# Routing over 112 sums, bank copies in runs of four, a third buffer for late rows, and three unused tiles

## The chip, the cores and the metric

The kernel runs on one core of a Trainium2 chip. A core has a matrix engine (TensorE, PE in the profile, with its weight loads as PEld), VectorE (DVE), ScalarE (ACT), GpSimd (POOL) and SyncE (SP, which here only issues DMAs), an on-chip memory SBUF of 128 partitions, and PSUM with eight banks for matmul results. Sixteen DMA engines move data between HBM and SBUF. The metric is the time of one execution on the device, in microseconds.

## The reference

One layer of a streaming encoder over 512 frames and 16 leading meta tokens, model width 2048: two attention branches (a latent attention with 8 heads and a stick-breaking attention with 8 heads), gated, merged and added to the input; then a layer of 16,384 tiny experts (PEER), a residual add and a final norm. The change touches the expert layer. For each token:

```python
q = (xb @ w_q).reshape(PEER_BLOCK, PEER_HEADS, 2, PEER_HALF)
s = jnp.einsum('thcd,hcnd->thcn', q, sub_keys).astype(jnp.float32)
s1, i1 = lax.top_k(s[:, :, 0], PEER_TOPK)
s2, i2 = lax.top_k(s[:, :, 1], PEER_TOPK)
cand_s = (s1[..., :, None] + s2[..., None, :]).reshape(PEER_BLOCK, PEER_HEADS, -1)
cand_i = (i1[..., :, None] * PEER_NKEYS + i2[..., None, :]).reshape(PEER_BLOCK, PEER_HEADS, -1)
top_s, top_pos = lax.top_k(cand_s, PEER_TOPK)
idx = jnp.take_along_axis(cand_i, top_pos, axis=-1)
g = jax.nn.softmax(top_s, axis=-1).reshape(PEER_BLOCK, -1)
h = jnp.einsum('tkd,td->tk', u[idx], xb)
act = (g * jax.nn.gelu(h.astype(jnp.float32), approximate=False)).astype(xb.dtype)
return jnp.einsum('tk,tkd->td', act, v[idx])
```

Both lists of 16 come sorted. A sum of places a and b (counted from 0) has (a+1)(b+1) sums that are at least as large, itself included. So a sum with a >= 4 and b >= 4 has at least 25 of them and need not be looked at; 4 x 16 + 12 x 4 = 112 sums are left.

## The kernel before

**Matmuls in three parts.** All weights and activations are fp32. `wtile` (line 213) loads a weight tile `wr` (128 partitions x 1024) on SP's DMA queue, rounds it on ACT into `wh` (line 223) and takes the rest on DVE into `wl` (line 224). Activations are kept split in the same way (`xh`/`xl`, `yh_`/`yl_`, `mgh`/`mgl`, `hgh`/`hgl`, `vah`/`val`). `mm3` (lines 235 to 237) issues three matmuls for each product, in which a 128x128 piece of the weight tile is the stationary operand. `wr` has four buffers, `wh` and `wl` three each, with one more pair for every fourth tile in the last two stages (`more["pool"]`).

**Stages.** First the projections of x with 512 or 264 columns (xh), then the attentions; the branch outputs (line 771, on yh_a and yh_b, 512 columns); the output projection (line 809, on mgh, 512 columns), which leaves `hgh`/`hgl`; the query projection for routing (line 960, on hgh, 512 columns), with the scores and the top 16 of each 128 (`top16`, line 859). Then the experts, and here the 512 tokens are treated in two ways. For 342 of them (ND) all 16,384 experts are computed densely: in `for e in range(NK)` (line 1213, 128 blocks of 48 matmuls with 342 columns) the products with u, and after it, by `STEPS` (line 1292), the products with v. Which experts count is laid on by a table of gates. For the other 170 tokens the chosen rows of u and v are gathered: 128 tokens have one partition each, and 42 tokens three partitions each.

**Rows.** `send` (line 1142) issues one gather of 128 rows of 2048 floats on POOL's queue, `row_step` (line 1163) lets DVE multiply such a row with the tokens and sum (for u, line 1171), or scale and add it (for v, line 1175). There are 171 u rows and 171 v rows, numbered through. `rows_due` (line 1207) issues row steps in pace with the position in the u loop, by the table

```python
PACE = (2, 14, 60, 124, NK - 0.5), (0, 10, 75, 173.5, NU)
```

so 173.5 rows are due at block 124 and NU = 179 at the end. `lead` says how many rows beyond the current one may have been sent: 4 or 6 in most of the loop, 2 from row 166 (OWN - 4) on. Up to row 169 the rows rotate through the buffers of three tags (rows, hin, gin); from row 170 (OWN) on only the two of `rw` are left, since hin and gin then hold the first groups of the v stage. In the v stage, every third row gets a tile of another pool (`gs["pool"]`), and the lead is 3.

**Routing and gates.** `route` (line 887) works through one tile of 128 tokens: sums (line 897), the best 16 of 256 for each head (line 901), and twice, for the two halves of the position, a one-hot comparison, a product and a sum (lines 909 to 913). It is a generator; each `yield` is a point where other work is issued. One token tile is routed under the scores (`early`, line 930, nine steps after every fourth block), three under the u loop (`routing`, line 1105). `gates_of` (line 1038) then builds, token by token, a 128 x 128 table of gates on TensorE (line 1074); `gate_out` (line 1082) copies four tokens of a PSUM bank with two ACT instructions (line 1095) into `gb`, from where POOL's queue stores it to DRAM. The v stage reads it back as `gin` and multiplies it to the stored `hin` (`gated`, line 1199).

**Order.** A scheduler orders each engine's instructions when the program is built. Instructions of one engine start in that order, so a DVE instruction that waits for a gather holds all later ones, the `wl` of line 224 among them.

Of the kernel before, what the change touches and what calls it, by code (L numbers as in the profile page):

```python
# [22 lines left out]
P = 128  # L23
# [39 lines left out]
def _constants():  # L63
    p = np.arange(P)
    cols = {
        "ident": np.eye(P),
        "ones": np.ones((P, P)),
        "tri": (p[:, None] >= p[None, :]),
        "perm": (p[:, None] == (p[None, :] ^ 32)),
        "neg": np.where(p[None, :] <= p[:, None], NEG, 0.0),  # L70
        "qlo": np.where(p[None, :] < 64, 1.0, 0.0) * np.ones((P, 1)),
        "negrow": np.full((P, 64), NEG),
        "freq": (10000.0 ** (-((p % 32) / 32.0)))[:, None],
        "sign": np.where(p % 64 < 32, -1.0, 1.0)[:, None],
        "iota": np.arange(TOPK)[None, :] * np.ones((P, 1)),
        "sel": (p[:, None] // RB == np.arange(NB)[None, :]),
        "eps": np.full((P, 1), EPS),
        "halfpi": np.full((P, 1), math.pi / 2),
    }
    out = []  # L80
    for part in range(2):
        arrs, o = [], 0
        for k, v in cols.items():
            if (k in MIXER_CONST) == bool(part):
                v = np.asarray(v, np.float64).astype(np.float32)
                CONST[k] = (part, o, o + v.shape[1])
                o += v.shape[1]
                arrs.append(v)
        out.append(np.ascontiguousarray(np.concatenate(arrs, axis=1)))
    return out  # L90
# [106 lines left out]
def body(tc, nc, a, dbg=None):  # L197
# [55 lines left out]
    gn = cp.tile([P, 56], F32, name="gn")  # L253
    SP.dma_start(gn, a["gains"])
    csts = [cp.tile([P, CONST_ARR[0].shape[1]], F32, name="cst")]

    def C(k):
        return csts[CONST[k][0]][:, CONST[k][1]:CONST[k][2]]
# [501 lines left out]
    for n, y in (("a", ya), ("b", yb)):  # L760
        yh_ = sp2.tile([P, H, SEQ], F32R, name=f"yh_{n}")
        yl_ = sp2.tile([P, H, SEQ], F32R, name=f"yl_{n}")
        for h in range(H):
            split(yh_[:, h], yl_[:, h], y[:, h])
        ys.append((yh_, yl_))
    mixer.close()
    merge = ExitStack()
    bp = merge.enter_context(tc.tile_pool(name="merge", bufs=1, side="left"))
# [25 lines left out]
    hgl = hgp.tile([P, KC, SEQ], F32R, name="hgl")  # L794
    rh_ = hgp.tile([P, SEQ], F32, name="rh_")
    gr_last = hgp.tile([P, 2, P], F32, name="gr_last")
    rcol = hgp.tile([P, 1], F32, name="rcol")
    rcolb = hgp.tile([P, 1], F32, name="rcolb")

# [53 lines left out]
    eob = rp.tile([P, KB], I32, name="eob")  # L853
    stage = ExitStack()
    rk = stage.enter_context(tc.tile_pool(name="rank", bufs=1, side="right"))
    v1 = rk.tile([P, 4, 16, TOPK], F32, name="v1")
    i1 = rk.tile([P, 4, 16, TOPK], U32, name="i1")

    def top16(vals, idx, src, n):
        wk = rk.tile([P, n], F32, name="wk", tag=f"wk{n}")  # L860
# [13 lines left out]
    def spread_rows():  # L874
# [9 lines left out]
        SP.dma_start(eob[:PB], eob_d.rearrange("t (r k) -> (t r) k", r=RB))  # L884
        SP.dma_start(gwb[:PB], gwb_d.rearrange("t (r k) -> (t r) k", r=RB))

    def route(ti, n, pool):
        shp = [P, n, TOPK, TOPK]
        tv = pool.tile([P, H, TOPK], F32, name="tv", bufs=1)
        ef = keys[ti] = pool.tile([P, 2, H, TOPK], F32, name="ef", bufs=1)  # L890
        for h0 in range(0, H, n):
            hs = slice(2 * h0, 2 * (h0 + n))
            vv, ii = (t[:, ti, hs].rearrange("p (h c) k -> p h c k", c=2) for t in (v1, i1))
            i1f = pool.tile([P, n, 2, TOPK], F32, name="i1f", bufs=1)
            V.tensor_copy(i1f, ii)
            cand = pool.tile([P, n, TOPK, TOPK], F32, name="cand", bufs=1)
            V.tensor_tensor(cand, vv[:, :, 0, :, None].to_broadcast(shp), vv[:, :, 1, None, :].to_broadcast(shp), ALU.add)
            yield
            tp = pool.tile([P, n, TOPK], U32, name="tp", bufs=1)
            for h in range(n):  # L900
                top16(tv[:, h0 + h], tp[:, h], cand[:, h].rearrange("p a b -> p (a b)"), 256)
                yield
            for c, (op_, arg) in enumerate(((ALU.logical_shift_right, 4), (ALU.bitwise_and, 15))):
                pu = pool.tile([P, n, TOPK], U32, name="pu", bufs=1)
                pf = pool.tile([P, n, TOPK], F32, name="pf", bufs=1)
                V.tensor_scalar(pu, tp, arg, None, op_)
                V.tensor_copy(pf, pu)
                oh = pool.tile([P, n, TOPK, TOPK], F32, name="oh", tag="cand", bufs=1)
                V.tensor_tensor(oh, pf[:, :, :, None].to_broadcast(shp), iota[:, None, None, :].to_broadcast(shp), ALU.is_equal)
                yield  # L910
                V.tensor_tensor(oh, oh, i1f[:, :, c, None, :].to_broadcast(shp), ALU.mult)
                yield
                V.reduce_sum(ef[:, c, h0:h0 + n], oh, axis=AX.X)
                yield
        e_ = pool.tile([P, H, TOPK], F32, name="e_", bufs=1)
        V.scalar_tensor_tensor(e_, ef[:, 0], float(NK), ef[:, 1], ALU.mult, ALU.add)
        ev = e_.rearrange("p h k -> p (h k)")
        if ti == 3:
            V.tensor_copy(eo, ev)
        gw = gw_all[:, ti].rearrange("p (h k) -> p h k", k=TOPK)  # L920
        V.tensor_tensor(gw, tv, tv[:, :, :1].to_broadcast(sh2), ALU.subtract)
        S.activation(gw, gw, AF.Exp)
        sm = pool.tile([P, H], F32, name="gsum", bufs=1)
        V.reduce_sum(sm, gw, axis=AX.X)
        V.reciprocal(sm, sm)
        V.tensor_tensor(gw, gw, sm[:, :, None].to_broadcast(sh2), ALU.mult)
        if ti == NT - 1:
            V.tensor_copy(er, ev)

    early = route(3, 2, rk)  # L930
    with tc.tile_pool(name="score", bufs=2, side="left") as sp_, \
# [9 lines left out]
        def scores(hc, qh, ql):  # L941
            ps = ps_tile()
            skh, skl = sk["now"]
            s = slice(hc % 8 * P, (hc % 8 + 1) * P)
            for ti in range(4):
                t = slice(ti * P, (ti + 1) * P)
                mm3(ps[:, t], qh[:, t], ql[:, t], skh[:, s], skl[:, s], True, True)
            sc = sp_.tile([P, 4, NK], F32, name="sc")
            S.activation(sc, ps.rearrange("p (t n) -> p t n", n=NK), AF.Copy)
            for ti in (3, 2, 0, 1):  # L950
                top16(v1[:, ti, hc], i1[:, ti, hc], sc[:, ti], NK)
            if hc % 4 == 3:
                for _ in range(9):
                    next(early, None)

        late = []
# [77 lines left out]
    def after_gelu(ins):  # L1034
        if "gelu" in more:
            tc.add_manual_dep(ins.ins, more["gelu"].ins.name, NOSYNC, reason="not before its block")
# [45 lines left out]
    def gate_out(hold=3):  # L1082

        for _ in range(min(2, len(banks))):
            if banks[0][1] % TB == 0 and len(banks) < hold:
                return
            ps, tok, w = banks.pop(0)
            b, o = tok // TB, tok % TB
            if o == 0:
                gb["now"] = [vi.tile([P, NK // 2, TB], F32, name="gb", tag="gin") for _ in range(2)]  # L1090
                if ND - tok < TB:
                    for half in gb["now"]:
                        G.memset(half[:, :, ND - tok:], 0.0)
            for hf, half in enumerate(gb["now"]):
                after_gelu(S.activation(half[:, :, o:o + w].rearrange("p i t -> p t i"),
                                        ps.rearrange("p (t f i) -> p f t i", t=4, f=2)[:, hf, :w], AF.Copy))
                if o + w == TB or tok + w == ND:
                    for q in range(2):
                        g0 = hf * NG // 2 + q * NG // 4
                        G.dma_start(g_d[g0:g0 + NG // 4, :, b].rearrange("g p j t -> p g (j t)"),  # L1100
                                    half[:, q * NK // 4:(q + 1) * NK // 4].rearrange("p (g j) t -> p g (j t)", j=GRP))
# [2 lines left out]

    def routing():
        for ti in (2, 0, 1):
            yield from route(ti, 2, rk)
            routed.append(ti)
            while routed:
                yield  # L1110
# [31 lines left out]
    def send():  # L1142
# [5 lines left out]
            tag = ("rows", "hin", "gin")[(n - gs["six"]) % 3]  # L1148
        else:
            tag = ("rows", "hin")[n % 2] if n < OWN else "rows"  # L1150
        if tag != "rows":
            row = vi.tile([P, D], F32, name="row", tag=tag)
        elif gs["pool"] is not None and n % 3 == 0:
            row = gs["pool"].tile([P, D], F32, name="row", bufs=1)
        else:
            row = rw.tile([P, D], F32, name="row")
# [50 lines left out]
    def rows_due(pos):  # L1207
        while gs["done"] < np.interp(pos, PACE[0], PACE[1]):
            n = gs["done"]
            row_step(more["lo"], 6 if gs["six"] is not None and gs["six"] + 4 <= n < OWN - 6 else 4 if n < OWN - 4 else 2)  # L1210

    more["pool"] = stage.enter_context(tc.tile_pool(name="weights_u", bufs=1, side="left"))
    for e in range(NK):
# [162 lines left out]
```

## Time and profile before

| | us |
|---|---|
| median of 3 runs | 3620.9 (3619.91 to 3624.22) |
| the profiled execution | 3625.05 |
| its span | 3623.3 |
| TensorE busy | 3571.3 |
| DVE busy | 2614.3 |
| ACT busy | 1469.4 |
| POOL busy | 708.3 |

The page gives, for one profiled execution, the busy time of each engine, the share of each engine and line in the chain of work that ended last, and groups of equal instructions with their count, busy time and mean; behind the second bar stands the idle time before them and what ended it. Matmuls overlap each other, so the durations of single ones add up to more than the span; their pace is read from their starts. A view of stretches gives the same engines for chosen pieces of the span, with the granted TensorE clock (1.00 is full), the mean share of the DMA engines that was busy, and GB/s.

### The profile page before, as it was taken

Reading aid. Unit: us, or ns where it says so; the run is one execution under the profiler, and the core shown is the slowest. Engines: PE = TensorE matmul, PEld = TensorE weight load, DVE = VectorE, ACT = ScalarE, POOL = GpSimd, SP = SyncE. Lnnn points to the kernel's source line nnn. Section 1 sums busy time; section 2 is a strip of 40 time slices with the busy share of each in tenths; the row PEclk is TensorE's granted clock in tenths of the full one; section 3 lists DMA queues with packets and bytes.
Section 4 is the critical chain, followed back from the end, with each engine's and each line's share of the span. In section 5 each row is a group of like instructions: output and inputs, shape, how many; then the busy total and the mean of one; then the engine's idle time right before and its main releaser. Section 6 shows DMA issues by size and latency. Waiting matters only on the chain.

```text
span 3623.3 us, 54294 instructions
## 1 busy us (share of the span) xinstructions
PE 3571.3 (99%) x21481; PEld 3302.7 (91%) x21481; DVE 2614.3 (72%) x3702; ACT 1469.4 (41%) x2334; POOL 708.3 (20%) x523
## 2 busy tenths in 40 slices
PE   9999999999999999999999999999999999999998
PEld 8988888888788887899999999999999999999997
DVE  5533344435554558799999988887688898898987
ACT  4233333334443233233676666664323333333333
POOL 1000000000011122112232222223232322332320
PEclk9999999999999999999999999999999999999998
DMA  4222222221144443268999999999899999999993
GB/s 170 98 100 100 93 95 96 93 105 47 37 139 134 146 140 112 98 231 324 345 366 362 361 372 372 361 373 383 328 383 343 388 394 374 368 384 358 386 347 121
DMA packets 218535, 890.04 MB, mean 246 GB/s; under 512 B 24660, under 2 KB 47528, under 8 KB 174504
## 3 DMA queue, kind: packets, MB, share of 16 engines
q1 hardware_dynamic: 133160, 462.87, 35.1%
q0 software_dynamic: 56608, 384.51, 27.2%
q10 hardware_dynamic: 28512, 39.20, 3.0%
q8 instruction: 168, 2.75, 0.3%
q14 instruction: 87, 0.71, 0.1%
HBM read 824.18 MB, written 62.30 MB: 245 GB/s over the span
## 4 chain that ended last, share of the span: by engine, by line
PE 75%; DMA 10%; issue 7%; DVE 6%; POOL 1%; ACT 0%; SPq 0%; DVEq 0%; POOLq 0%; ACTq 0%
PE ps L235 24%; PE ps L236 23%; PE ps L237 23%; DMA row<-v,eo 5%; DMA hin<-h_d 2%; DVE xg L1175 2%; PE ps L1074 2%; DVE wl L224 1%; POOL row L1158 1%; DMA wr<-vb 1%; DVE val L241 0%; DMA row<-v,eob 0%; PE ps L714 0%; DMA gin<-g_d 0%; DVE acc L1346 0%
## 5 line engine op out<-in xcount | busy, mean ns | idle before, releaser
L223 ACT ACTIVATE wh<-wr 128x1024 fp32r<-128x1024 f32 (+1 forms) x756 | 796.1, 1056 | 1580.7 <-PE ps L237 1306.4
L224 DVE TENSOR_TENSOR wl<-wr,wh 128x1024 fp32r<-128x1024 f32 (+1 forms) x741 | 937.4, 1271 | 400.7 <-ACT wh L223 399.0
L235 PE MATMUL ps<-hgh,wl 128*128 128x342 f32 (+1 forms) x2304 | 772.9, 335 | 9.0 <-DVE wl L224 6.8
L236 PE MATMUL ps<-hgl,wh 128*128 128x342 f32 (+1 forms) x2304 | 759.4, 330 | 0.9 <-DVE hgl L241 0.7
L237 PE MATMUL ps<-hgh,wh 128*128 128x342 f32 (+1 forms) x2304 | 756.2, 328 | 0.0
L235 PE MATMUL ps<-vah,wl 128*128 128x342 f32 x2048 | 657.0, 321 | 12.5 <-DVE wl L224 12.5
L236 PE MATMUL ps<-val,wh 128*128 128x342 f32 x2048 | 654.4, 320 | 0.0
L237 PE MATMUL ps<-vah,wh 128*128 128x342 f32 x2048 | 653.0, 319 | 0.0
L235 PE MATMUL ps<-xh,wl 128*128 128x512 f32 (+1 forms) x1376 | 470.3, 342 | 5.8 <-ACT xh L329 5.8
L236 PE MATMUL ps<-xl,wh 128*128 128x512 f32 (+1 forms) x1376 | 470.2, 342 | 0.2 <-DVE xl L330 0.2
L237 PE MATMUL ps<-xh,wh 128*128 128x512 f32 (+1 forms) x1376 | 468.0, 340 | 0.0
L235 PEld LDWEIGHTS ps<-hgh,wl 128*128 128x128 f32 x2304 | 438.8, 190 | 22.1 <-DVE wl L224 8.2
L236 PEld LDWEIGHTS ps<-hgl,wh 128*128 128x128 f32 x2304 | 436.0, 189 | 11.0 <-DVE hgl L241 1.9
L237 PEld LDWEIGHTS ps<-hgh,wh 128*128 128x128 f32 x2304 | 434.4, 189 | 11.1 <-issue 0.2
L235 PEld LDWEIGHTS ps<-vah,wl 128*128 128x128 f32 x2048 | 386.3, 189 | 15.1 <-DVE wl L224 15.0
L236 PEld LDWEIGHTS ps<-val,wh 128*128 128x128 f32 x2048 | 387.8, 189 | 0.0
L237 PEld LDWEIGHTS ps<-vah,wh 128*128 128x128 f32 x2048 | 386.4, 189 | 0.0
L1175 DVE SCALAR_TENSOR_TENSOR xg<-row,act,xg 128x2048 f32<-128x2048 f32 x127 | 298.1, 2347 | 41.0 <-DMA row<-v,eo 41.0
L1158 POOL DMA_INDIRECT row<-v,eo x128 | 219.9, 1718 | 547.2 <-DVE xg L1175 487.6
L1171 DVE SCALAR_TENSOR_TENSOR row<-row,xg 128x2048 f32<-128x2048 f32 x128 | 292.4, 2284 | 3.9 <-DMA row<-u,eo 3.8
L235 PEld LDWEIGHTS ps<-xh,wl 128*128 128x128 f32 x1376 | 259.5, 189 | 38.1 <-ACT xh L329 6.5
L236 PEld LDWEIGHTS ps<-xl,wh 128*128 128x128 f32 x1376 | 259.2, 188 | 31.7 <-DVE xl L330 1.0
(474 smaller groups left out, 4702.2 us busy)
## 6 DMA issues: line engine op xcount, KB each, us to landing
wr<-ut SPq DMA_DIRECT2D x256, 512.0 KB, 7.3
wr<-vb SPq DMA_DIRECT2D x256, 512.0 KB, 7.0
wr<-front SPq DMA_DIRECT2D x238, 512.0 KB, 3.5
g_d<-gb POOLq DMA_DIRECT2D x44, 512.0 KB, 10.6
gin<-g_d SPq DMA_DIRECT2D x32, 704.0 KB, 8.1
h_d<-hb ACTq DMA_DIRECT2D x128, 171.0 KB, 6.7
hin<-h_d SPq DMA_DIRECT2D x32, 684.0 KB, 7.3
gates<-gt ACTq DMA_DIRECT2D x32, 256.0 KB, 2.0
```

What stands on the lines that cost most here:

```text
L223: more["last"] = S.activation(hi[:, s], raw[:, s], AF.Copy)
L224: more["lo"] = (eng or V).tensor_sub(lo[:, s], raw[:, s], hi[:, s].bitcast(F32))
L235: T.matmul(ps, wl, xh, start=start, stop=False)
L236: T.matmul(ps, wh, xl, start=False, stop=False)
L237: T.matmul(ps, wh, xh, start=False, stop=stop)
L1074: T.matmul(bank[:, o:o + P], ohs[(p - 2) % 3][:, 1, :, t], x, start=c == 0, stop=c == 2)
L1158: G.indirect_dma_start(out=row, out_offset=None, in_=a[src], in_offset=bass.IndirectOffsetOnAxis(ap=idx, axis=0))
L1171: ins = V.scalar_tensor_tensor(row, row, 1.0, x, ALU.mult, ALU.mult, accum_out=w)
L1175: ins = V.scalar_tensor_tensor(y, row, w, y, ALU.mult, ALU.add)
```

## The change

Five things are changed:

- `route` forms 112 sums instead of 256: the first 4 of list one with all 16 of list two, and the other 12 with the first 4. The place of a chosen sum is turned back into its two list places: the first by comparing it with the starts of the 16 runs (constant `first`), where the differences of neighbouring keys (`step`) are summed; the second by a mask and a correction for runs of four. Under the u loop four heads are handled at once instead of two, with the wide instructions still over two.
- The bank copies of `gate_out` run over tokens innermost, so that they write runs of four floats and read PSUM with a stride, where they read runs of 64 and wrote with a stride before.
- `v1` and `i1`, the sorted lists, become two halves of one tile `lists`. Once they are used up, every third row from 170 to 178 is gathered into it (172, 175, 178), and the lead there is 3 instead of 2.
- The early routing takes ten steps at a time instead of nine.
- Three tiles that nothing uses are allocated (`pad`, `pad2`, `pad3`: 160, 160 and 96 bytes of each partition), and the constants grow by 16 columns (64 bytes). This moves other tiles. In the built programs the start of a tile in its partition, modulo 256 bytes, is:

| tile | before | after |
|---|---|---|
| wr, wh, wl | 96 | 64 |
| mgh, mgl | 96 | 64 |
| yh_a, yl_a, yh_b, yl_b | 224 | 64 |
| hgh, hgl | 160 | 64 |
| row, hin, gin | 160 | 128 |
| xh, xl | not moved | not moved |

```diff
+        "first": np.where(np.arange(TOPK) < 4, 16 * np.arange(TOPK), 48 + 4 * np.arange(TOPK))[None, :] * np.ones((P, 1)),
...
+    cp.tile([P, 40], F32, name="pad")
...
+    sp2.tile([P, 40], F32, name="pad2")
...
+    hgp.tile([P, 24], F32, name="pad3")
...
-    v1 = rk.tile([P, 4, 16, TOPK], F32, name="v1")
-    i1 = rk.tile([P, 4, 16, TOPK], U32, name="i1")
+    lists = rk.tile([P, D], F32, name="lists")
+    v1, i1 = (lists[:, c * D // 2:(c + 1) * D // 2].rearrange("p (t h k) -> p t h k", t=4, h=16) for c in range(2))
+    i1 = i1.bitcast(U32)
...
-            cand = pool.tile([P, n, TOPK, TOPK], F32, name="cand", bufs=1)
-            V.tensor_tensor(cand, vv[:, :, 0, :, None].to_broadcast(shp), vv[:, :, 1, None, :].to_broadcast(shp), ALU.add)
+            cand = pool.tile([P, 512], F32, name="cand", bufs=1)[:, :n * 112].rearrange("p (h x) -> p h x", x=112)
+            for x0, a0, na, nb in ((0, 0, 4, 16), (64, 4, 12, 4)):
+                V.tensor_tensor(cand[:, :, x0:x0 + na * nb].rearrange("p h (a b) -> p h a b", b=nb),
+                                vv[:, :, 0, a0:a0 + na, None].to_broadcast([P, n, na, nb]),
+                                vv[:, :, 1, None, :nb].to_broadcast([P, n, na, nb]), ALU.add)
+
+            step = pool.tile([P, 4, TOPK], F32, name="step", bufs=1)[:, :n]
+            V.tensor_copy(step[:, :, :1], i1f[:, :, 0, :1])
+            V.tensor_sub(step[:, :, 1:], i1f[:, :, 0, 1:], i1f[:, :, 0, :TOPK - 1])
             yield
...
-                top16(tv[:, h0 + h], tp[:, h], cand[:, h].rearrange("p a b -> p (a b)"), 256)
+                top16(tv[:, h0 + h], tp[:, h], cand[:, h], 112)
                 yield
...
+            V.tensor_copy(pf, tp)
+            V.tensor_scalar(pu, tp, 15, None, ALU.bitwise_and)
+            V.tensor_copy(pb, pu)
+            V.tensor_scalar(pu, tp, 12, None, ALU.bitwise_and)
+            V.tensor_copy(p12, pu)
+            V.scalar_tensor_tensor(p12, pf, 64.0, p12, ALU.is_ge, ALU.mult)
+            V.tensor_sub(pb, pb, p12)
+            yield
+            for c, (place, table, op_) in enumerate(((pf, C("first"), ALU.is_ge), (pb, iota, ALU.is_equal))):
+                for h in range(0, n, 2):
...
-                for _ in range(9):
+                for _ in range(10):
                     next(early, None)
...
-                after_gelu(S.activation(half[:, :, o:o + w].rearrange("p i t -> p t i"),
-                                        ps.rearrange("p (t f i) -> p f t i", t=4, f=2)[:, hf, :w], AF.Copy))
+                after_gelu(S.activation(half[:, :, o:o + w],
+                                        ps.rearrange("p (t f i) -> p f i t", t=4, f=2)[:, hf, :, :w], AF.Copy))
...
-            yield from route(ti, 2, rk)
+            yield from route(ti, 4, rk)
...
-        if tag != "rows":
+        if OWN <= n < NU and (n - OWN) % 3 == 2:
+            row = lists
+        elif tag != "rows":
...
-            row_step(more["lo"], 6 if gs["six"] is not None and gs["six"] + 4 <= n < OWN - 6 else 4 if n < OWN - 4 else 2)
+            row_step(more["lo"], 6 if gs["six"] is not None and gs["six"] + 4 <= n < OWN - 6 else 4 if n < OWN - 4 else 3)
```

More of the change, by code (lines that the diff above doesn't have):

```diff
@@ L887, in route @@
     def route(ti, n, pool):
-        shp = [P, n, TOPK, TOPK]
+        shp = [P, 2, TOPK, TOPK]
         tv = pool.tile([P, H, TOPK], F32, name="tv", bufs=1)
@@ L893, in route @@
             vv, ii = (t[:, ti, hs].rearrange("p (h c) k -> p h c k", c=2) for t in (v1, i1))
-            i1f = pool.tile([P, n, 2, TOPK], F32, name="i1f", bufs=1)
+            i1f = pool.tile([P, 4, 2, TOPK], F32, name="i1f", bufs=1)[:, :n]
             V.tensor_copy(i1f, ii)
-            cand = pool.tile([P, n, TOPK, TOPK], F32, name="cand", bufs=1)
-            V.tensor_tensor(cand, vv[:, :, 0, :, None].to_broadcast(shp), vv[:, :, 1, None, :].to_broadcast(shp), ALU.add)
+            cand = pool.tile([P, 512], F32, name="cand", bufs=1)[:, :n * 112].rearrange("p (h x) -> p h x", x=112)
@@ L898, in route @@
             yield
-            tp = pool.tile([P, n, TOPK], U32, name="tp", bufs=1)
+            tp = pool.tile([P, 4, TOPK], U32, name="tp", bufs=1)[:, :n]
             for h in range(n):
-                top16(tv[:, h0 + h], tp[:, h], cand[:, h].rearrange("p a b -> p (a b)"), 256)
+                top16(tv[:, h0 + h], tp[:, h], cand[:, h], 112)
                 yield
[L903 to L914, printed above, removed]
+            pf, pb = (pool.tile([P, 4, TOPK], F32, name=x, bufs=1)[:, :n] for x in ("pf", "pb"))
@@ new lines, in route @@
+            tmp = pool.tile([P, 512], F32, name="tmp", tag="cand", bufs=1)[:, :2 * n * TOPK]
+            tmp = tmp.rearrange("p (c h k) -> p c h k", c=2, k=TOPK)
+            pu, p12 = tmp[:, 0].bitcast(U32), tmp[:, 1]
+            V.tensor_copy(pf, tp)
[4 more added lines that the diff above has]
+            V.scalar_tensor_tensor(p12, pf, 64.0, p12, ALU.is_ge, ALU.mult)
@@ new lines, in route @@
+            V.tensor_sub(pb, pb, p12)
+            yield
+            for c, (place, table, op_) in enumerate(((pf, C("first"), ALU.is_ge), (pb, iota, ALU.is_equal))):
+                for h in range(0, n, 2):
+                    oh = pool.tile([P, 512], F32, name="oh", tag="cand", bufs=1).rearrange("p (h k a) -> p h k a", h=2, k=TOPK)
+                    key = step[:, h:h + 2] if c == 0 else i1f[:, h:h + 2, 1]
+                    V.tensor_tensor(oh, place[:, h:h + 2, :, None].to_broadcast(shp), table[:, None, None, :].to_broadcast(shp), op_)
+                    yield
+                    V.tensor_tensor(oh, oh, key[:, :, None, :].to_broadcast(shp), ALU.mult)
+                    yield
+                    V.reduce_sum(ef[:, c, h0 + h:h0 + h + 2], oh, axis=AX.X)
+                    yield
```

## The prediction

> **What bounds the kernel now.** I read the page first, then equal stretches of the span, then single matmuls, then the waits.
>
> ```profile
> span 3623.3 us, 54294 instructions
> PE 3571.3 (99%) x21481; PEld 3302.7 (91%) x21481; DVE 2614.3 (72%) x3702; ACT 1469.4 (41%) x2334; POOL 708.3 (20%) x523
> PE ps L235 24%; PE ps L236 23%; PE ps L237 23%; DMA row<-v,eo 5%; DMA hin<-h_d 2%; DVE xg L1175 2%; PE ps L1074 2%; DVE wl L224 1%; POOL row L1158 1%; DMA wr<-vb 1%; DVE val L241 0%; DMA row<-v,eob 0%; PE ps L714 0%; DMA gin<-g_d 0%; DVE acc L1346 0%
> ```
>
> TensorE is busy for 99% of the span, and the three split matmuls are 70% of the chain that ended last. So a saving on DVE, ACT or POOL is worth nothing unless TensorE was waiting for it. Two things can still be gained: TensorE's pace, and the places where it stops.
>
> The stretches (microseconds, TensorE busy and matmuls in brackets, then the other engines, granted clock, DMA share, GB/s) show where it stops:
>
> ```profile
> 1050.00:1150.00 100.00, 100.00 (x432) 81.08 (x431) 48.05 (x45) 35.48 (x44) 11.60 (x9) 1.00 0.44 142
> 2500.00:2600.00 100.00, 96.37 (x601) 95.80 (x600) 74.76 (x62) 31.05 (x38) 22.39 (x16) 0.98 0.94 367
> 2600.00:2700.00 100.00, 90.54 (x552) 89.70 (x551) 78.48 (x68) 30.04 (x29) 28.49 (x15) 0.95 0.93 355
> 3100.00:3200.00 100.00, 100.00 (x639) 100.00 (x638) 88.28 (x74) 31.59 (x30) 30.06 (x18) 1.00 0.96 372
> ```
>
> An undisturbed 100 us holds 639 matmuls of 342 columns (156.5 ns each), with the DMA engines at 0.96. From 2500 to 2700, where the u experts end and the v experts begin, 38 + 87 = 125 are missing: 125 x 156.5 = 19.6 us.
>
> TensorE's pace is read from the starts of L235 matmuls, three matmuls apart each:
>
> ```profile
> 200.38 0.40 PE L235 MATMUL ps<-xh,wl 128*128 128x512 f32 x1
> ...
> 205.94 0.40 PE L235 MATMUL ps<-xh,wl 128*128 128x512 f32 x1
> 1224.82 0.39 PE L235 MATMUL ps<-mgh,wl 128*128 128x512 f32 x1
> ...
> 1229.58 0.39 PE L235 MATMUL ps<-mgh,wl 128*128 128x512 f32 x1
> 1423.91 0.39 PE L235 MATMUL ps<-hgh,wl 128*128 128x512 f32 x1
> ...
> 1425.97 0.39 PE L235 MATMUL ps<-hgh,wl 128*128 128x512 f32 x1
> 1639.93 0.32 PE L235 MATMUL ps<-hgh,wl 128*128 128x342 f32 x1
> ...
> 1645.53 0.32 PE L235 MATMUL ps<-hgh,wl 128*128 128x342 f32 x1
> 2252.53 0.32 PE L235 MATMUL ps<-hgh,wl 128*128 128x342 f32 x1
> ...
> 2255.37 0.32 PE L235 MATMUL ps<-hgh,wl 128*128 128x342 f32 x1
> ```
>
> 512 columns take 5.56/24 = 231.7 ns on xh, 4.76/21 = 226.7 on mgh, 2.06/9 = 228.9 on hgh, and on yh the first stretch above gives 100/432 = 231.5. 342 columns on hgh take 5.60/36 = 155.6 early and 2.84/18 = 157.8 later. The shape and the granted clock (1.00) are the same, so the pace depends on something else. The built program offers a candidate, the start of the moving tile minus that of the split weight, modulo 256 bytes. Weights wh and wl start at 96 (modulo 256); mgh and mgl at 96, difference 0, the fastest; hgh and hgl at 160, difference 64, the middle; yh and yl at 224, difference 128, slow; xh and xl run through 0, 64, 128 and 192, slow on the mean.
>
> **The change part by part.** *The unused tiles.* With the 16 added columns of constants they move wh, wl, mgh, mgl, yh, yl, hgh and hgl all to 64 modulo 256: difference 0 everywhere but in x, whose four become 32, 96, 160 and 224. I take the mgh pace for what becomes difference 0.
>
> ```profile
> L235 PE MATMUL ps<-hgh,wl 128*128 128x342 f32 x2048 | 670.6, 327 | 6.8 <-DVE wl L224 6.8
> L235 PE MATMUL ps<-hgh,wl 128*128 128x512 f32 x256 | 102.4, 400 | 2.2 <-ACT hgh L240 2.2
> L235 PE MATMUL ps<-yh_a,wl 128*128 128x512 f32 x128 | 50.6, 395 | 1.2 <-ACT yh_a L240 1.2
> ```
>
> Each group stands three times (L235, L236, L237), yh for a and b. Branch outputs: 2 x 3 x 128 = 768 matmuls x (231.5 - 226.7) = 3.7 us. Queries: 768 x (228.9 - 226.7) = 1.7 us. u experts: 3 x 2048 = 6144 matmuls; I let the early pace of 155.6 hold for the first 20 of the 128 blocks (960 matmuls), up to where the gates' matmuls begin, so 5184 x g. No row has 342 columns at difference 0 throughout; g is bounded from above by the whole gap to the fastest other pace (the mgh step seen against yh, 4.8 ns: 25 us) and from below by a loss as large as yh against hgh, -2.6 ns (-13 us). I take 228.9 - 226.7 = 2.2 ns, the same step from 64 to 0 at the nearest shape; it also leads to 155.6, a pace this stage has shown. 5184 x 2.2 = 11.4 us. The x projections (2112 matmuls of 512 columns): between all at 226.7 (-10.6 us) and slower by the step from mgh to hgh, 2.2 ns (+4.6 us); I take 0, since no row shows these differences, and the 264-column ones pass through the same eight residues before and after. The v experts keep their differences: 0. DMA packets are as many and as long: 0. Sum 16.8 us.
>
> *The third buffer.* These rows are DVE's waits from 2500 to 2660 us, TensorE's up to 2565 and from there to 2660, the landing of all gathers, then DVE and POOL in order of time:
>
> ```profile
> DVE xg L1175 <- DMA row<-v,eo: 21.1, 7, 5.7
> PE ps L235 <- DVE wl L224: 1.6, 1, 1.6
> PE ps L235 <- DVE wl L224: 11.5, 4, 6.6
> DMA to landing us min/median/max: 5.3/9.0/17.5
> 2570.22 2.35 DVE L1175 SCALAR_TENSOR_TENSOR xg<-row,act,xg 128x2048 f32<-128x2048 f32 x1 [2.24 <-DMA row<-v,eo]
> 2581.67 2.35 DVE L1175 SCALAR_TENSOR_TENSOR xg<-row,act,xg 128x2048 f32<-128x2048 f32 x1 [4.56 <-DMA row<-v,eo]
> 2629.47 2.35 DVE L1175 SCALAR_TENSOR_TENSOR xg<-row,act,xg 128x2048 f32<-128x2048 f32 x1 [5.68 <-DMA row<-v,eo]
> 2638.60 4.62 DVE L224 TENSOR_TENSOR wl<-wr,wh 128x1024 fp32r<-128x1024 f32 x4
> 2621.61 1.43 POOL L1158 DMA_INDIRECT row<-v,eo  x1 [11.98 <-DMA acc<-ht_d]
> ```
>
> DVE works in order, so wl splits queue behind a row that has not landed, and TensorE waits for wl. Two buffers give a row every (9.0 + 2.35)/2 = 5.7 us; the pace table wants 5.5 rows in 3.5 blocks of 48 x 157.8 ns, one per 4.8 us. Three give one per 3.8 us. With a lead of 3, row 180 also leaves the pool tile whose gather waited 11.98 us, and the 5.68 us behind it, with four splits late at 2638, should go. TensorE's 1.6 us come before DVE's first wait for a v row (2570) and stay; of the 11.5 behind it I take 11 us. The ends are 0 (the gathers only delay the weight loads, DMA share 0.93) and 19.6 - 1.6 = 18.0 us (the lower clock of that stretch, 0.95, goes too). Late next are the weight loads themselves, for which ACT waits 47.6 us in the same place:
>
> ```profile
> ACT wh L223 <- DMA wr<-ut: 47.6, 17, 7.7
> ```
>
> POOL issues as many gathers in the same order; nothing else queues on it there.
>
> *Routing.* Per head, the five selection instructions:
>
> ```profile
> L862 DVE FIND_INDEX8 tp<-tv,cand 128x8 uint32<-128x256 f32 x32 | 13.4, 420 | 0.0
> L862 DVE FIND_INDEX8 i<-v,sc 128x8 uint32<-128x128 f32 x64 | 18.3, 285 | 0.0
> L897 DVE TENSOR_TENSOR cand<-v 128x512 f32<-128x512 f32 x16 | 11.0, 687 | 0.0
> L907 DVE CAST pf<-pu 128x32 f32<-128x32 uint32 x32 | 5.7, 178 | 0.5
> L1095 ACT ACTIVATE gb<-ps 128x256 f32<-128x256 f32 x170 | 92.5, 672 | 0.0
> ```
>
> 128 elements more cost 135 ns; at 112 instead of 256 an instruction saves 152 ns: 32 heads x 5 x 152 = 24 us. The sums go from 16 x 687 to about 7 us (-4); some 20 more small instructions at 0.18 us cost 4; the 96 wide one-hot instructions stay. 24 us less on DVE, three quarters of it under u experts. TensorE runs through 1600 to 2500 without a stop, so this is worth 0. The number of yields per token tile, 36, and with it the order around the splits, stays (40 against 36 in the early one, matched by ten steps).
>
> *Bank copies.* L1095's 114 us of ACT (170 x 672 ns): the write gets runs of four, the read of PSUM a stride of 128 elements instead. Between 0.4 and 0.9 us each; nothing on TensorE's path waits for them: 0.
>
> Sum: 16.8 + 11 = 27.8 us. The profiled execution took 3625.05 us (span 3623.3), 4.15 above the median of the runs, 3620.9; on the median: 3593.
>
> **The rivals.** *The addresses do nothing*: mgh is faster for another reason (its stage loads no gates). For it: the 342-column pace changes from 155.6 to 157.8 with no address changed. Against: the ordering 0, 64, 128 at one shape. 3620.9 - 11 = 3610. The Trainium skill's page SBUF — State Buffer, section Who interferes with whom, has it that "PE and ACT never wait on anyone"; by that, moving tiles could not change TensorE's pace. This trace has equal matmuls at unequal paces under one clock, though it cannot show the address to be the cause.
>
> *The third buffer is worth nothing*: DMA at 0.93 to 0.94 is the limit, and a gather more in flight makes wr later by what the rows come earlier. For it: ACT's 47.6 us. 3620.9 - 16.8 = 3604.
>
> *Neither does anything*: 3621.
>
> *Equal starts are the worst, not the best*: moving rows and weights meet in the same place, and everything at difference 0 runs as slowly as yh. Then mgh loses 768 x 4.8 = 3.7 us, queries 768 x 2.6 = 2.0, u experts 6144 x 2.6 = 16.0; against the buffer's 11 that is +10.7: 3632. It decides from +0.9 ns on the u experts (6144 x 0.9 = 5.5, with 5.7 elsewhere, against 11). Against it stands mgh; for it, that a 342-column row repeats at another phase than a 512-column one.
>
> **How the numbers follow.** Both parts work: 0.47, 3593, own range 3575 (18 us at the buffer, x at mgh's pace: 3620.9 - 16.8 - 18.0 - 10.6) to 3604. Addresses nothing 0.16; buffer nothing 0.12; neither 0.08; equal starts slow 0.17. A difference under 0.2% (7 us) can't be told from none here. Faster by more: 0.47 + 0.16 + 0.12 = 0.75; same 0.08; slower 0.17. The range leaves out the last case and the far lower end: 3577 to 3626.
>
> **What would show it.** L235 starts on yh and on hgh at 512 columns 226.7 ns apart, on hgh at 342 columns 155.6 or less at 2200 us. About 620 matmuls or more in each 100 us around the last u block, DVE's waits for row<-v well under 21 us there, no 12 us wait on POOL. Selection on 112 sums at 260 to 270 ns with TensorE's stops unchanged. It would be wrong if the pace on hgh rose, if x slowed, or if the weight loads took over the stop at the turn.

## The result and the profile after

The changed kernel takes 3609.7 us (median of 6 runs, 3606.21 to 3613.96) beside 3620.4 us for the kernel before on the same chip (6 runs). The ratio is 0.9967, 95% interval 0.9953 to 0.998: faster by 11.9 us (7 to 17) by that ratio. Forecast were 27.8. The sign and the range held, the size did not. The profiled execution took 3613.96 us, 4.3 above its median, as the one of before was 4.15 above its own, so the two can be laid side by side.

The page of the changed kernel, span, engines and chain:

```profile
span 3612.2 us, 54318 instructions
PE 3562.8 (99%) x21481; PEld 3298.8 (91%) x21481; DVE 2593.9 (72%) x3726; ACT 1432.4 (40%) x2334; POOL 704.6 (20%) x523
PE ps L236 27%; PE ps L237 27%; PE ps L238 26%; PE ps L1101 2%; DMA wr<-vb 1%; DVE wl L225 1%; DMA hin<-h_d 1%; DMA row<-v,eo 1%; DVE xg L1204 1%; DMA wr<-ut 1%; POOL row L1187 1%; DMA row<-v,eob 0%; PE ps L717 0%; DMA row<-u,eo 0%; DVE xgb
```

The lines of the split matmuls are now L236 to L238. TensorE is as much the bound as before; DVE and ACT lost 20.4 and 37 us of busy time, which is not where the gain came from (e5 below). The same stretches as in the prediction:

```profile
1050.00:1150.00 100.00, 100.00 (x443) 82.81 (x442) 49.75 (x47) 36.69 (x46) 12.95 (x10) 1.00 0.44 142
2500.00:2600.00 100.00, 97.86 (x611) 97.57 (x610) 74.69 (x60) 32.38 (x40) 16.62 (x14) 0.98 0.96 370
2600.00:2700.00 100.00, 94.37 (x582) 93.81 (x581) 80.15 (x70) 31.28 (x29) 24.33 (x15) 0.97 0.95 361
3100.00:3200.00 100.00, 100.00 (x639) 100.00 (x638) 89.33 (x75) 33.03 (x31) 24.29 (x18) 1.00 0.95 365
```

The branch outputs hold 443 matmuls in 100 us instead of 432. The turn from the u to the v experts (second and third row) holds 1193 instead of 1153: 40 x 156.5 ns = 6.3 us won there, and 85 matmuls are still missing against twice 639. Now single matmuls, on yh, on hgh with 512 columns, and on hgh with 342 columns early and late, each pair 27, 12, 36 and 18 matmuls apart:

```profile
1011.65 0.39 PE L236 MATMUL ps<-yh_b,wl 128*128 128x512 f32 x1
...
1017.77 0.39 PE L236 MATMUL ps<-yh_a,wl 128*128 128x512 f32 x1
1422.61 0.39 PE L236 MATMUL ps<-hgh,wl 128*128 128x512 f32 x1
...
1425.33 0.39 PE L236 MATMUL ps<-hgh,wl 128*128 128x512 f32 x1
1639.78 0.32 PE L236 MATMUL ps<-hgh,wl 128*128 128x342 f32 x1
...
1645.46 0.32 PE L236 MATMUL ps<-hgh,wl 128*128 128x342 f32 x1
2252.55 0.31 PE L236 MATMUL ps<-hgh,wl 128*128 128x342 f32 x1
...
2255.39 0.31 PE L236 MATMUL ps<-hgh,wl 128*128 128x342 f32 x1
```

6.12/27 = 226.7 ns on yh and 2.72/12 = 226.7 on hgh: both 512-column paces are the ones forecast. 5.68/36 and 2.84/18 = 157.8 on hgh with 342 columns: the later u experts did not move, and the 155.6 of their first blocks is gone. The waits from 2500 to 2660 us:

```profile
DVE xg L1204 <- DMA row<-v,eo: 7.9, 5, 4.1
PE ps L236 <- DVE wl L225: 7.6, 2, 5.5
ACT wh L224 <- DMA wr<-ut: 39.6, 14, 5.6
ACT wh L224 <- DMA wr<-vb: 22.5, 4, 10.6
POOL row L1187 <- DMA acc<-ht_d: 15.3, 1, 15.3
```

DVE waits 7.9 us for v rows, and 1.0 for one that lands in `lists`, instead of 21.1; TensorE waits 7.6 for wl instead of 13.1. ACT's waits for wr are the longest of these (39.6 + 22.5 us), but TensorE's own longest stop still stands behind a late row:

```profile
2606.56 1.25 POOL L1187 DMA_INDIRECT row<-v,eo  x1 [0.30 <-issue]
2606.77 1.06 ACT L224 ACTIVATE wh<-wr 128x1024 fp32r<-128x1024 f32 x1 [1.48 <-PE ps L238]
2615.74 2.35 DVE L1204 SCALAR_TENSOR_TENSOR xg<-row,act,xg 128x2048 f32<-128x2048 f32 x1 [4.08 <-DMA row<-v,eo]
2622.26 4.62 DVE L225 TENSOR_TENSOR wl<-wr,wh 128x1024 fp32r<-128x1024 f32 x4
2623.53 0.66 PE L236 MATMUL ps<-vah,wl 128*128 128x342 f32 x1 [5.45 <-DVE wl L225]
```

ACT had finished the wh for the first of the four wl splits at 2607.83. DVE, which works in order, then waited 4.08 us for a row and came to the splits at 2622.26; 5.45 of TensorE's 7.6 us follow from that. The same picture stands in the profiles of e2 and e3 (rows 4.03 and 3.49 us late, TensorE stopped for 5.55 and 5.09). POOL's long wait did not go either: it moved to the gather of a row that is needed only at 2636.38, but the gather of the late row, issued at 2606.56, stands right behind it in POOL's queue. DVE had finished with that row's buffer at 2603.88, so up to 2.7 us of the row's lateness can come from there; no run separates it. The edited instructions themselves:

```profile
L868 DVE FIND_INDEX8 tp<-tv,cand 128x8 uint32<-128x112 f32 x32 | 8.6, 267 | 0.0
L1122 ACT ACTIVATE gb<-ps 128x256 f32<-128x256 f32 x170 | 52.6, 372 | 0.0
```

A selection over 112 sums takes 267 ns (forecast 260 to 270), a bank copy 372 ns, just under the 0.4 to 0.9 us allowed for.

### The profile page after: what moved, and what is told of

It reads as the page before. It is cut to its first block, busy times and chain, and to the rows that moved or that the text cites. A ratio compares the mean times of both kernels' runs of the same rounds, so it can differ in the third digit from the quotient of the medians.

```text
span 3612.2 us, 54318 instructions
## 1 busy us (share of the span) xinstructions
PE 3562.8 (99%) x21481; PEld 3298.8 (91%) x21481; DVE 2593.9 (72%) x3726; ACT 1432.4 (40%) x2334; POOL 704.6 (20%) x523
## 4 chain that ended last, share of the span: by engine, by line
PE 85%; DMA 5%; DVE 4%; issue 4%; POOL 1%; ACT 1%; DVEq 0%; SPq 0%; POOLq 0%; ACTq 0%
PE ps L236 27%; PE ps L237 27%; PE ps L238 26%; PE ps L1101 2%; DMA wr<-vb 1%; DVE wl L225 1%; DMA hin<-h_d 1%; DMA row<-v,eo 1%; DVE xg L1204 1%; DMA wr<-ut 1%; POOL row L1187 1%; DMA row<-v,eob 0%; PE ps L717 0%; DMA row<-u,eo 0%; DVE xgb L1204 0%
## 5 line engine op out<-in xcount | busy, mean ns | idle before, releaser
L236 PE MATMUL ps<-hgh,wl 128*128 128x342 f32 (+1 forms) x2304 | 770.8, 335 | 5.4 <-DVE wl L225 3.2
L238 PE MATMUL ps<-hgh,wh 128*128 128x342 f32 (+1 forms) x2304 | 751.5, 326 | 0.0
L236 PE MATMUL ps<-vah,wl 128*128 128x342 f32 x2048 | 658.4, 321 | 13.7 <-DVE wl L225 13.7
L238 PE MATMUL ps<-vah,wh 128*128 128x342 f32 x2048 | 654.1, 319 | 0.0
L236 PE MATMUL ps<-xh,wl 128*128 128x512 f32 (+1 forms) x1376 | 471.3, 343 | 5.3 <-ACT xh L332 5.3
L238 PE MATMUL ps<-xh,wh 128*128 128x512 f32 (+1 forms) x1376 | 469.6, 341 | 0.0
L236 PEld LDWEIGHTS ps<-hgh,wl 128*128 128x128 f32 x2304 | 435.9, 189 | 16.9 <-DVE wl L225 4.0
L237 PEld LDWEIGHTS ps<-hgl,wh 128*128 128x128 f32 x2304 | 434.7, 189 | 11.4 <-DVE hgl L242 1.9
L238 PEld LDWEIGHTS ps<-hgh,wh 128*128 128x128 f32 x2304 | 434.5, 189 | 10.5 <-issue 0.2
L236 PEld LDWEIGHTS ps<-vah,wl 128*128 128x128 f32 x2048 | 387.2, 189 | 17.1 <-DVE wl L225 17.1
L238 PEld LDWEIGHTS ps<-vah,wh 128*128 128x128 f32 x2048 | 387.4, 189 | 0.0
L1187 POOL DMA_INDIRECT row<-v,eo x125 | 204.7, 1637 | 545.9 <-DVE xg L1204 491.6
L1204 DVE SCALAR_TENSOR_TENSOR xg<-row,act,xg 128x2048 f32<-128x2048 f32 x124 | 290.8, 2345 | 25.3 <-DMA row<-v,eo 25.3
L236 PEld LDWEIGHTS ps<-xh,wl 128*128 128x128 f32 x1376 | 259.6, 189 | 36.8 <-ACT xh L332 5.3
```

The costliest lines, as they stand in the source:

```text
L236: T.matmul(ps, wl, xh, start=start, stop=False)
L237: T.matmul(ps, wh, xl, start=False, stop=False)
L238: T.matmul(ps, wh, xh, start=False, stop=stop)
L1187: G.indirect_dma_start(out=row, out_offset=None, in_=a[src], in_offset=bass.IndirectOffsetOnAxis(ap=idx, axis=0))
L1204: ins = V.scalar_tensor_tensor(y, row, w, y, ALU.mult, ALU.add)
```

## The experiments

**One part at a time.** My theory after the traces: the buffer gave most of the gain, the tiles only the 512-column part, and in the u experts the difference of starts does not do what it does at 512 columns. The rival: the tiles work, and the routing edits spoil the u pace. The ratios of all experiments are against the kernel before on the same chip, where no other is named.

*e1, the unused tiles alone*, on the kernel before; 56 columns stand for the tile of 40 and the 16 added constants, so that every TensorE operand starts where it does after the change:

```diff
+    cp.tile([P, 56], F32, name="pad")
...
+    sp2.tile([P, 40], F32, name="pad2")
...
+    hgp.tile([P, 24], F32, name="pad3")
```

> The three unused tiles alone, on the kernel before; every TensorE operand starts where it starts in the changed kernel. If the tiles carry what the trace of the changed kernel suggests (branch outputs -4.4 us, queries and their scores -4.0, x +1.3, first u blocks +2.0, the rest of u pace +0.3 ns x 5184 = +1.6), about -4 to -6 us against before and a u-expert pace of 157.6 ns from the first block on. If the forecast's term was right and the other edits spoilt the u pace: 155.6 ns or less and -17 us.

Measured: 0.9993 (0.9984 to 1.0001), -2.5 us (-5.8 to +0.4): all tiles together can't be told from none in the time. The u experts run at 157.6 ns from the first block on, without any routing edit: the rival falls.

*e2, the third buffer alone*, on the kernel before, addresses of TensorE's operands as before:

```diff
+    lists = rk.tile([P, D], F32, name="lists")
+    v1, i1 = (lists[:, c * D // 2:(c + 1) * D // 2].rearrange(...) for c in range(2))
...
+        if OWN <= n < NU and (n - OWN) % 3 == 2:
+            row = lists
...
-            row_step(more["lo"], ... else 4 if n < OWN - 4 else 2)
+            row_step(more["lo"], ... else 4 if n < OWN - 4 else 3)
```

> The third buffer of late rows and the lead of three alone, addresses of TensorE's operands as before. If the traces' difference at the turn (block 120 to the first v matmul: 71.0 to 64.5 us) is the buffer's: -6 to -7 us. By the forecast: -11. If the turn is bound by DMA and the gain in the changed kernel came from the other edits: 0.

Measured: 0.9971 (0.996 to 0.9983), -10.5 us (-14.5 to -6.2). Its stretches at the turn, and its wait for v rows from 2500 to 2660 us:

```profile
2500.00:2600.00 100.00, 98.53 (x625) 98.24 (x624) 79.53 (x65) 32.20 (x40) 21.58 (x16) 1.00 0.98 380
2600.00:2700.00 100.00, 94.45 (x585) 93.94 (x584) 81.08 (x71) 31.65 (x30) 24.09 (x15) 0.97 0.94 362
```

```profile
DVE xg L1178 <- DMA row<-v,eo: 5.8, 4, 4.0
```

1210 matmuls instead of 1153: 57 x 156.5 ns = 8.9 us. The turn varies from execution to execution: these two rows sum to 1143, 1149 and 1162 in the other profiles without the buffer (e12, e1, e5), and to 1207 in e3 with it. The 6.3 us seen in the changed kernel's own profile is at the low end of what the buffer gives. DMA was at 0.94 to 0.98 all the same, so the share of busy DMA engines did not forbid the gain. One more thing changed in e2 and in the changed kernel: the first of the three rows of `lists` is not gathered at the turn at all. Its gather was issued as soon as the sorted lists were used up, at 1940.03 us (changed kernel) and 1997.78 (e2), though its row step comes at 2559.18 and 2565.19:

```profile
1940.03 0.94 POOL L1187 DMA_INDIRECT lists<-v,eo  x1 [0.31 <-DVE cand L907]
```

So the turn has one gather fewer as well as one buffer and a longer lead, and e2 holds all three together.

*e5, routing and bank copies alone*: the changed kernel without the buffer, with tiles that give every difference of starts as before:

```diff
-    cp.tile([P, 40], F32, name="pad")
...
-    sp2.tile([P, 40], F32, name="pad2")
+    sp2.tile([P, 48], F32, name="pad2")
...
-    hgp.tile([P, 24], F32, name="pad3")
+    hgp.tile([P, 48], F32, name="pad3")
...
-        if OWN <= n < NU and (n - OWN) % 3 == 2:
-            row = lists
-        elif tag != "rows":
+        if tag != "rows":
...
-            row_step(more["lo"], ... else 4 if n < OWN - 4 else 3)
+            row_step(more["lo"], ... else 4 if n < OWN - 4 else 2)
```

> The routing over 112 sums and the bank copies in runs of four, without the third buffer and with every difference of starts (modulo 256) as before the change. Forecast: 0 (-24 us on VectorE, -51 us on ScalarE, both beside TensorE). If they carry part of the changed kernel's gain, or take some of it away: beyond -0.2% or +0.2%. The first 20 u blocks run at 155.6 or at 157.8 ns, whichever of the two repeating patterns they fall into.

Measured: 1.0004 (0.9995 to 1.0013): nothing. The three parts sum to -2.5 - 10.5 + 1.4 = -11.6 us, the whole is -11.9: within their intervals the parts add.

**How the difference of starts acts.** The changed kernel with other sizes of the three unused tiles, so that hgh and hgl start at another distance behind wh and wl, modulo 256 bytes (sizes are rounded up to 32 bytes). yh and mgh stay at 0.

```diff
 e3:     hgp.tile([P, 8], ..., "pad3")
 e4:     cp.tile([P, 8], ..., "pad");  sp2.tile([P, 72], ..., "pad2")
 e9:     cp.tile([P, 8], ..., "pad");  sp2.tile([P, 72], ..., "pad2");  hgp.tile([P, 12], ..., "pad3")
 e7:     cp.tile([P, 8], ..., "pad");  sp2.tile([P, 72], ..., "pad2");  hgp.tile([P, 8], ..., "pad3")
 e8:     cp.tile([P, 8], ..., "pad");  sp2.tile([P, 72], ..., "pad2");  no "pad3"
```

> The changed kernel with the hg tiles 64 bytes higher, so that they start 64 bytes (modulo 256) behind the split weights, as before the change. If the difference of starts sets the pace of the u experts: 155.6 ns again in the first 20 blocks and 157.8 behind them, 512 columns at 229.1; total within 2 us of the changed kernel (-2.0 and -1.9 in u against +2.3 in the queries). If the start of the stage or the routing edit set it: 157.6 from the first block on and 227.5 at 512 columns.

> The changed kernel with the hg tiles 128 bytes (modulo 256) behind the weights, yh and mgh still at 0. At 512 columns 231.5 to 232.4 ns as yh had it at 128 (before), 768 x 4.9 = +3.7 us against the changed kernel. At 342 columns no run shows it: if the ordering of 512 columns (0, 64, 128: faster to slower) held, over 158 ns and at least +2.5 us; if 342 columns follow another rule, anything from 154 to 160 ns, 6144 x -3.6 to +2.4 = -22 to +15 us.

> The changed kernel with the hg tiles 160 bytes (modulo 256) behind the weights. Pace of the u experts so far: 157.6 (0), 157.8 or 155.6 (64), 159.8 (128), 155.0 (192), 155.1 (224); of 512 columns 227.5, 229.2, 232.7, 233.3, 233.3. If both shapes change smoothly with the difference: 342 columns between 155 and 160 ns, 512 columns at 233. If 342 columns are already as fast as at 192: 155.0 and a total near 3602.

> The changed kernel with the hg tiles 192 bytes (modulo 256) behind the weights. 512 columns took 227.5, 229.2 and 232.7 ns at 0, 64 and 128; 342 columns 157.6, 157.7 and 159.8. If the difference acts symmetrically (192 like 64): 229 and 157.7 or 155.6. If it acts in one direction (192 worst): over 232.7 and over 159.8.

> The changed kernel with the hg tiles 224 bytes (modulo 256) behind the weights, that is 32 ahead of them. If it acts symmetrically: between the values at 0 and 64, 227.5 to 229.2 and 157.6. If the 342-column pace, whose rows end at another phase (1368 bytes), has its best somewhere else than at 0: toward 154 to 156 ns in the u experts, -10 to -20 us.

Measured; paces are the mean distance of two starts on hgh in each trace, distances with a stop in them (over 253 and 182 ns, other matmuls in between among them) left out, and the blocks are timed from start to start. e7 and e8 ran twice each:

| difference | kernel | 512 columns, ns | 342 columns, ns | u blocks 20 to 112, us | ratio to before |
|---|---|---|---|---|---|
| 0 | changed | 227.5 | 157.6 | 767.3 | 0.9967 |
| 64 | e3 | 229.2 | 157.8 | 769.0 | 0.9963 |
| 128 | e4 | 232.7 | 159.8 | 775.2 | 0.9995 |
| 160 | e9 | 234.2 | 159.6 | 777.3 | 1.0008 |
| 192 | e7 | 233.3 | 155.0 | 756.7 | 0.9938 |
| 224 | e8 | 233.3 | 155.1 | 756.6 | 0.9939 |

The difference sets the pace at both shapes, but not in the same way. At 512 columns 0 is the best and 192 and 224 are among the worst; at 342 columns 0 and 64 are alike and 192 and 224 are the best. The lines of e4 and of e8 in the u experts, 36 matmuls apart, in this order:

```profile
1640.06 0.32 PE L236 MATMUL ps<-hgh,wl 128*128 128x342 f32 x1
...
1645.82 0.32 PE L236 MATMUL ps<-hgh,wl 128*128 128x342 f32 x1
```

```profile
1640.15 0.32 PE L236 MATMUL ps<-hgh,wl 128*128 128x342 f32 x1
...
1645.79 0.32 PE L236 MATMUL ps<-hgh,wl 128*128 128x342 f32 x1
```

5.76/36 = 160.0 ns against 5.64/36 = 156.7 (at 224 the pace alternates, and this pair lies in its slower part). On hgh it is the difference and not the place: at 64 the weights started at 96 (before), 64 (e3) and 160 (e5) modulo 256, and 512 columns took 229.1, 229.2 and 229.2 ns. The x projections do not follow the differences alone: their four are 32, 96, 160 and 224 in the changed kernel and in e4 and e7 to e9, with the weights at 64 and at 192, and their 512 columns take 232.8 and 232.3 ns.

**Where the early 155.6 ns came from.** At difference 64 three kernels (e2, e3, e5) had 157.8 ns from the first u block on, and before had 155.6 there. So the kernel before was profiled once more, unchanged.

> The kernel before, unchanged, profiled a second time. Its first profile had 155.6 ns in the first 20 u blocks and 157.8 behind them; the third buffer alone and the routing alone, with the same difference of starts, had 157.8 from the first block on. If the pattern hangs on the phase in which the stage happens to start: 157.8 may show here too, with no edit at all, and the block starts 2.0 us later. If the two edits moved it: 155.6 again in blocks 0 to 18.

Measured: 1.0005 (0.999 to 1.0019). From 1600 to 1700 us, the second profile of the kernel before, and then its first one:

```profile
1600.00:1700.00 100.00, 100.00 (x636) 100.00 (x635) 99.10 (x175) 36.58 (x44) 17.32 (x15) 1.00 0.87 326
```

```profile
1600.00:1700.00 100.00, 100.00 (x645) 100.00 (x644) 99.11 (x178) 35.68 (x43) 18.43 (x15) 1.00 0.88 329
```

636 and 645 matmuls in the same 100 us of one and the same kernel, at the same granted clock. In both traces every three starts of this stage are either 466.7 or 473.3 ns apart for blocks on end, and at full clock they change from one to the other only behind an interruption of the sequence (a stop, or other matmuls in between), as where the gates' matmuls begin or end. At difference 64 there are thus two repeating patterns. That the phase in which TensorE starts again decides which one holds is my reading; no run sets that phase. At difference 0 single sums of three run from 461 to 480 and average 472 to 474 in every block; at 224 nearly all are 460 or 470.

**Does it hold in another stage?** In the v experts rows of 342 columns followed each other without a gap, so each row had another difference. e10 pads the rows to 384 columns and puts all but the first of the 32 groups at 192; e11 adds e7's tiles.

```diff
-        parts[g] = [vp.tile([P, GRP, ND], F32R, name=x, bufs=3) for x in ("vah", "val")]
+        parts[g] = [vp.tile([P, GRP, 384], F32R, name=x, bufs=3)[:, :, :ND] for x in ("vah", "val")]
...
+    vp.tile([P, 32], F32, name="pad4", bufs=1)
+    more["pool"].tile([P, 56], F32, name="pad5")
```

> The changed kernel with the v experts' moving rows padded from 342 to 384 columns (1536 bytes, a multiple of 256), and two unused tiles that put every row 192 bytes (modulo 256) behind all its weights; before, each row had another difference. If the difference of starts sets the pace in this stage as it did in u at 192: 155.0 instead of 157.2 ns, 6144 x 2.2 = -13.5 us against the changed kernel. If the DMA engines, at 0.96 there, can't give more: 157.2 ns on the mean with more stops for wr<-vb, between 0 and -5 us. If u's values don't carry over: 0 or slower.

> As e10, and the hg tiles 192 bytes behind the weights as in e7. If the two add up: -9 (e7 against the changed kernel) and e10's gain; with e10 at -13.5 some 3587 to 3590 us on a chip where before takes 3623. If DMA takes the place of TensorE's pace as the bound: less than the sum, and no less than e7's 3602 if the v experts gain nothing.

Measured: e10 0.9939 (0.9925 to 0.9953), e11 0.9916 (0.9901 to 0.9931), 3593.67 us where before took 3625.22. e11 beats both kernels. The v experts of e10, then of e11, and the u experts of e11:

```profile
3100.00:3200.00 100.00, 100.00 (x645) 100.00 (x644) 87.97 (x74) 32.43 (x31) 22.86 (x17) 1.00 0.95 368
```

```profile
3100.00:3200.00 100.00, 99.89 (x651) 99.61 (x651) 90.63 (x75) 32.55 (x31) 38.90 (x18) 1.00 0.96 367
1600.00:1700.00 100.00, 100.00 (x649) 99.97 (x648) 96.01 (x179) 37.06 (x44) 21.32 (x15) 1.00 0.90 332
```

645 and 651 instead of 639 in the v experts, 649 instead of 637 in the u experts. The pace carried over: 155.4 ns (e10) and 154.9 (e11) where 157.2 were. Of e10's 13.5 us about 10 arrived ((0.9967 - 0.9939) x 3623); TensorE's waits for wl from 2610 to 3600 us are 17.5 us there and 13.7 in the changed kernel, so, by one profile of each, a part was given back in stops.

**What is left at the turn.** e6 loads less there; two thirds of h are left out of the output of six chunks.

```diff
-    begun, done = {}, {STAY[0] * 2 + c for c in range(4)} | set(range(6, 12)), []
+    begun, done = {}, {STAY[0] * 2 + c for c in range(4)}, []
...
-                residual(RES[at], acc[:, RES[at]], slice(0, SEQ))
+                residual(RES[at], acc[:, RES[at], ND:], slice(ND, SEQ))
```

> The changed kernel with the six residual loads at the turn cut from 512 to 170 columns: 6 x 128 x 342 x 4 bytes = 1.05 MB less to move between the u and the v experts (the rest of h is left out of the output of chunks 6 to 11). If the turn is now bound by the DMA engines: 1.05 MB at the 367 GB/s of that stretch, -2.9 us, block 120 to the 32nd v chunk 195.4 to about 192.5 us, and less waiting for wr<-vb (22.5 us). If late rows are still the limit, or only the order of the queue: 0.

Measured: 0.9965 (0.9951 to 0.9978) against 0.9967 for the changed kernel: no gain that can be told from none, but 2.9 us, as expected if the bytes were the bound, would lie within the intervals too. In its profile block 120 to the 32nd v chunk is 191.0 us instead of 195.4, but that stretch is 191.3 in e2 and 192.8 in e3, which load everything. Its late row is still there (2.64 us, TensorE stopped for 3.86 behind it). How much of the rest of the turn is the late row, how much the bytes and how much the order of the loads stays open.

## Why the prediction was wrong, step by step

*The step that failed* is the u experts' term of the unused tiles: "5184 x 2.2 = 11.4 us". The true size is (768.6 - 767.3) = 1.3 us in blocks 20 to 112 (before; changed kernel), start to start, and nothing clear in the blocks ahead of them: 152.7 to 153.6 us at difference 0 (changed kernel, e1, e6, e10), 153.2 to 153.4 at 64 (e2, e3, e5, e12), and 150.7 in the one profile with 155.6. Both of its reasons fell. The step from 64 to 0 was read at 512 columns and carried to 342; at 342 columns it is 0.2 ns, and the order of the differences is another one (e3, e4, e7 to e9). And 155.6, "a pace this stage has shown", was not the pace of a condition that 0 would restore, but one of two patterns at 64, present in one profile of the kernel and absent in the next (e12). One profile was read as a property of the kernel.

*Branch outputs and queries*, -3.7 and -1.7: right. 768 x (232.4 - 226.7) = 4.4 and 768 x (229.1 - 227.5) = 1.2 us, from the mean paces of the two traces.

*The x projections*, 0 with bounds -10.6 and +4.6: 231.8 became 232.8, 2112 x 1.0 = +2.1 us, inside the bounds. Sum of the tiles by these: -4.4 - 1.2 + 2.1 - 1.3 = -4.8 us; e1 measured -2.5 (-5.8 to +0.4). Forecast were -16.8. Of the 16.8 the u experts' term was 11.4 and is where most of the forecast was lost.

*The third buffer*, -11 with bounds 0 and -18: right. e2 measured -10.5 (-14.5 to -6.2). The mechanism is in the main the one given: DVE waits less for late rows, and wl is split earlier. Four details were off. One row stays late, and TensorE's longest stop is behind it, not behind a weight load. POOL's wait behind acc<-ht_d stayed (15.3 us), ahead of that row's gather. POOL's gathers were not "in the same order": one moved out of the turn to 1940 us. And the stretches at the turn hold 611 and 582 matmuls in the changed kernel, not 620.

*Routing and bank copies*, 0: right, with the cover that was named (e5).

*The rivals.* "The addresses do nothing" gave 3610, and 3609.7 is the time. That it meets it is luck: the starts do change paces, but those chosen here nearly cancel (e1). The addresses change the pace of the branch outputs and queries, and a different choice of them is worth some 10 us more ((0.9967 - 0.9938) x 3620, e7, with two runs, against the changed kernel). What that rival had for it, a 342-column pace that changes with no address changed, was the sign that should have stopped me from carrying the term over. The Trainium skill's sentence quoted in the prediction (page SBUF — State Buffer, section Who interferes with whom), that "PE and ACT never wait on anyone", does not cover this: the changed kernel and e7 differ only in the sizes of unused tiles, and u blocks 20 to 112 take 767.3 and 756.7 us. "Equal starts are the worst" fell: neither of the two shapes is slowest at 0.

## What to carry to other kernels

A pace read at one tile shape does not price another shape: measure the shape that carries the most matmuls, here 12,288 of 342 columns (3 x 2048 in u and in v) against 768 in the stage that gave the number. Before a difference within one profile is taken for a property of the kernel, profile the same kernel twice. When TensorE is the bound, sweeping where its moving tiles start behind its weights takes only unused tiles and padded rows, and was worth more here than the change itself: e11 is 30 us faster than before (25 to 36), of which the change has 12.

## What the hardware did that was not expected

TensorE's pace at a granted clock of 1.00 varies with the distance from the split weights to the moving tile modulo 256 bytes: 226.7 to 234.2 ns at 512 columns, 155.0 to 159.8 at 342, with different orders (table). At some distances it locks into repeating patterns (sums of three 466.7 or 473.3 ns at 64, 460 or 470 at 224), and at full clock every change between them in the traces of before, e12, e3 and e8 stands behind an interruption of the sequence. Why 342 columns prefer 192 and 224 was not found. Laying the x projections' rows at one distance was not tried.
